# Forgetting attention without the row's constant and from the last block to the first, low key parts over zeros, and four output projection units in two pairs

## The chip, the cores and the metric

The kernel runs on one core of a Trainium2 chip. Its five engines run their own instruction queues: TensorE (PE: matmuls and transposes, with weight loads, PEld, beside them), VectorE (DVE), ScalarE (ACT), GpSimd (POOL) and SyncE (SP, which issues most DMAs). The metric is the device time of one execution, in microseconds; the time before is the median of three runs.

## The reference, cut to what matters

One decoder layer over 512 tokens of width 2048: a mixer, a cross-attention, a gated MLP, each behind an RMSNorm. The mixer has 12 dilated attention heads (A), 8 forgetting heads (B) and 4 heads of gated linear attention (C); their outputs, 2048 wide, go through one output projection. The forgetting heads:

```python
def forgetting_attention(q, k, v, f_logit):
    c = jnp.cumsum(jax.nn.log_sigmoid(f_logit.astype(jnp.float32)), axis=1)
    ...
    def block(args):                         # a block of 128 queries
        n, qn, cn = args
        logits = jnp.einsum('bihd,bjhd->bhij', qn, k, ...) * HEAD_DIM ** -0.5
        logits = logits + (cn[..., :, None] - cT[..., None, :])
        qpos = n * BLOCK_Q + jnp.arange(BLOCK_Q)
        logits = jnp.where(kpos[None, :] <= qpos[:, None], logits, -jnp.inf)
        p = jax.nn.softmax(logits, axis=-1)
        return jnp.einsum('bhij,bjhd->bihd', p.astype(v.dtype), v)
    ...
# hybrid_mixer:
    mixed = jnp.concatenate([o_a..., o_b..., o_c...], axis=-1)
    return mixed @ w_out
```

The term `cn` is one constant for each query, that is for each row of a softmax, and a softmax doesn't change when a constant is added to its row.

## The kernel before

**Products.** A float32 operand is split into a rounded high part and a low remainder (`xhi`/`xlo`, `whi`/`wlo`), ACT writing the high one and DVE the low one, and `mm3` (L375 to L377) issues three matmuls for each product of 128x128 weights with up to 512 columns: high by high, high by low, low by high. Tiles named `acc` are the PSUM accumulators of these foreground products, four in turn; all other PSUM tiles (`psS` scores, `psT` transposes, `psO` outputs) share four buffers of another tag.

**Foreground and background.** The foreground runs units: one unit takes a 128x1024 piece of weights by one DMA on SP (`wraw`), splits it in two halves and issues 24 matmuls. Attention heads, gates and the like are Python generators in `self.bg`; `tick` after every 12 foreground matmuls advances the first two of them by `self.rate` steps, one step being what stands between two `yield`s. PE instructions of a generator are put behind the last foreground matmul issued (`behind`). So the order on every engine is made by the generators' steps, and a scheduler orders the instructions of an engine from there.

**A head** (`attend`, L514 to L581). First step: query and key of the head are laid out over 128 partitions, `kh` with the rounded key in both halves (L526, L527) and `kl` with the low remainder in both (L529 by DVE, L530 a copy by ACT). Then eight steps, `scores` and `turn` of four blocks of 128 queries; block t has 128(t + 1) keys. `scores(t)`: two matmuls (L544, L545), one DVE operation that adds the bias and finds the row's maximum (L547), ACT's exponential with the row's sum (L548), a reciprocal (L549) and the scaling (L550). `turn(t)`: t + 1 transposes (L557), then `pth` by ACT (L565) and `ptl` by DVE (L566), at most two blocks at a time. The last step multiplies with the values (`psO`, L576 and L577) and writes the mixed stream (L579, L580).

**The bias of a forgetting head** (`bias_b`). `cb` (tile name `ba`) is the row of negative cumulative sums, the same in all partitions; for each block DVE makes a tile `bb`: `cb` minus the query's own constant `ci` (L599, L600), with the causal mask `self.tri` added to the last 128 columns (L600). The constants come from `forget`, which after the scan transposes the sums by four small PE transposes (L708) into `cnat` (L711). Five empty steps stand between scan and transposes.

**The gates** (`gates`): four heads' matmuls (L678), each followed by a DVE chain; they run as background together with `forget`, and `rel_bias` (L738) follows. **The output projection** has 16 units of two halves (`out_units`): the first halves of units 0 to 3 run while the last forgetting heads are in the background, the second halves behind them. Mixed tile k is split when a unit first asks for it (`mtile`).

Of the kernel before, what the change touches and what calls it, by code (L numbers as in the profile page):

```python
# [12 lines left out]
F32 = mybir.dt.float32  # L13
F32R = mybir.dt.float32r
I32 = mybir.dt.int32
AF = mybir.ActivationFunctionType
ALU = mybir.AluOpType
AX = mybir.AxisListType

P = 128  # L20
D = 2048
KT = D // P
S = 512
NT = S // P
# [3 lines left out]
DH = 64  # L28
A_HEADS = 12
B_HEADS = 8  # L30
# [37 lines left out]
PTB = 4  # L68
WR = 5
# [23 lines left out]
SB = 2  # L93
# [140 lines left out]
class _Trunk:  # L234
# [143 lines left out]
        if mark:  # L378
            self.last = last

    def out_units(self, src, nt, xs, evac, n=S):
        box = {}
        halves = len(xs) // 8

        def unit(half):
            if half == 0:
                box["ps"] = self.acc()
            w = self.weights(src[nt * halves + half])
            for kk in range(8):
                k = half * 8 + kk  # L390
                wh, wl = w(kk * P, P)
                self.mm3(box["ps"][:, :n], wh, wl, xs[k][0], xs[k][1], k == 0, k == len(xs) - 1)
                if kk == 3:
                    self.tick()
            if half == halves - 1:
                evac(box["ps"])

        return [lambda h=h: unit(h) for h in range(halves)]

# [118 lines left out]
    def attend(self, qf, kf, e, vv, bias_of, head, mix):  # L518
# [2 lines left out]
        o = slice(DH - DH * e, 2 * DH - DH * e)  # L521
        qs = ab.tile([P, S], F32R, name="qs", tag="qs", bufs=SB)
        kh = ab.tile([P, S], F32R, name="kh", tag="kh", bufs=SB)
        kl = ab.tile([P, S], F32R, name="kl", tag="kl", bufs=SB)
        nc.scalar.activation(qs[a], qf[a], AF.Copy)
        nc.scalar.activation(kh[a], kf[a], AF.Copy)  # L526
        nc.scalar.activation(kh[o], kf[a], AF.Copy)  # L527
        nc.vector.tensor_tensor(qs[o], qf[a], qs[a].bitcast(F32), op=ALU.subtract)
        nc.vector.tensor_tensor(kl[a], kf[a], kh[a].bitcast(F32), op=ALU.subtract)  # L529
        nc.scalar.activation(kl[o], kl[a].bitcast(F32), AF.Copy)  # L530
        yield
        pth = ab.tile([P, 1280], F32R, name="pth", tag="pth", bufs=PB)
        ptl = ab.tile([P, 1280], F32R, name="ptl", tag="ptl", bufs=PB)
# [32 lines left out]
                    nc.vector.tensor_tensor(lv, tv, hv.bitcast(F32), op=ALU.subtract)  # L566

        for f, t in ((scores, 0), (scores, 1), (turn, 0), (scores, 2), (turn, 1), (scores, 3), (turn, 2), (turn, 3)):
            f(t)
            yield  # L570
        po = self.pst("O")
        for b in range(NT):
# [17 lines left out]
    def bias_b(self, h):  # L590
        nc = self.nc
        cb = self.ab.tile([P, S], F32, name="ba", tag="ba", bufs=2)
        nc.scalar.dma_start(out=cb, in_=bass.AP(self.cdr.tensor, self.cdr.offset + h * S, [[0, P], [1, S]]))

        def get(t):
            b = self.ab.tile([P, P * (t + 1)], F32, name="bb", tag="pt", bufs=PTB, padded_shape=[P, S])
            ci = self.cnat[:, t, h:h + 1]
            if t:
                nc.vector.tensor_scalar(b[:, :P * t], cb[:, :P * t], ci, None, op0=ALU.subtract)  # L599
            nc.vector.scalar_tensor_tensor(b[:, P * t:], cb[:, P * t:P * (t + 1)], ci, self.tri,  # L600
                                           op0=ALU.subtract, op1=ALU.add)
            return b

        return get

# [80 lines left out]
    def forget(self):  # L686
        nc, gl = self.nc, self.pre
        fb = self.con.tile([B_HEADS, 1], F32, name="fb")
        with self.tc.issue_after(self.begun.ins):
            nc.gpsimd.dma_start(out=fb, in_=self.d["f_bias"])  # L690
        tp = self.pst("T")
        for t in range(NT):
            nc.tensor.transpose(tp[:B_HEADS, t * P:(t + 1) * P], self.fg[:, t, :B_HEADS], self.ident)
        z = gl.tile([B_HEADS, S], F32, name="fz", tag="zs", bufs=1)
        nc.vector.tensor_scalar(z, tp[:B_HEADS, :], fb, None, op0=ALU.add)
        n = self.neg_log_sigmoid(z, [B_HEADS, S])
        one = gl.tile([B_HEADS, S], F32, name="fone", tag="zs", bufs=1)
        nc.gpsimd.memset(one, 1.0)
        cn = gl.tile([B_HEADS, S], F32, name="cn")
        nc.vector.tensor_tensor_scan(cn, one, n, 0.0, ALU.mult, ALU.add)  # L700
        self.cdr = self.dr.tile([B_HEADS, S], F32, name="cdr")
        nc.scalar.dma_start(out=self.cdr, in_=cn)
        for _ in range(5):
            yield
        tq = self.pst("T")
        with self.behind():
            for t in range(NT):
                nc.tensor.transpose(tq[:, t * B_HEADS:(t + 1) * B_HEADS], cn[:, t * P:(t + 1) * P],  # L708
                                    self.ident[:B_HEADS, :B_HEADS])
        self.cnat = self.con.tile([P, NT, B_HEADS], F32, name="cnat")  # L710
        nc.vector.tensor_copy(self.cnat, tq[:, :NT * B_HEADS].rearrange("p (t h) -> p t h", h=B_HEADS))  # L711
        yield

    def rel_bias(self):
# [178 lines left out]
    def mixer(self):  # L893
# [91 lines left out]
        es_gl.close()  # L985
        self.mab = self.pool(self.es, "mab", "left")
        self.ab = self.pool(es_ab, "ab", "right")
        self.up_pre = {}
        for f in range(2, EARLY):
            self.up_sums(f)  # L990
# [18 lines left out]
        def evac_o(dt):  # L1009
            def f(ps):  # L1010
                self.resid(dt, ps, None, sqs, lambda n: self.mp.tile([P, n], F32, name="sqt", tag="sqt", bufs=2))
            return f
# [5 lines left out]
            def __getitem__(s, k):  # L1018
                return mtile(k)

        units = [self.out_units(d["w_o"], n, Lazy(), evac_o(n)) for n in range(KT)]
        self.rate = W_O / 2
        for n in range(4):
            units[n][0]()
            self.tick()
        self.rate = 0
        self.flush()
        es_ab.close()
# [832 lines left out]
```

## Time and profile before

| | |
|---|---|
| median of three runs | 2253.88 us (2253.62 to 2257.49) |
| the profiled execution | 2255.07 us, of which the span is 2253.3 us |
| busy PE / DVE / ACT / POOL | 2233.6 / 1824.1 / 1243.1 / 220.8 us |
| mean granted TensorE clock | 0.998 of full speed |
| gates and cumulative sums | 50 to 75 us of the span |
| dilated and forgetting heads | 330 to about 685 us |
| first halves of output units 0 to 3 | about 640 to 680 us |

Times count from the span's start. Matmuls are pipelined: one of 512 columns is shown with about 0.39 us, though the next starts 0.23 us later, so waits are read both from the idle time shown and from start to start. Idle time of an engine is put down to the last releaser. A line such as `psT<-ident,pt` reads output, arrow, inputs.

### The profile page before, as it was taken

What the parts mean: (1) busy time and instruction counts of PE and PEld (TensorE: products, weight loads), DVE (VectorE), ACT (ScalarE), POOL (GpSimd) and SP (SyncE); (2) the same over time, 40 slices, a digit from 0 to 9 for tenths busy, and PEclk for the clock granted to TensorE, in tenths of its full rate; (3) what the DMA queues carried; (4) which work ended last, traced back from release to release, by engine and by line L of the source; (5) the groups of instructions that cost most, each with busy time, mean ns of one, the idle gap of its engine ahead of it and who ended that gap; (6) DMA issues with size and microseconds to landing.
All of it is one profiled execution on the core that took longest, in us unless ns stands there. A gap on an engine that the chain in (4) does not pass through costs nothing.

```text
span 2253.3 us, 42653 instructions
## 1 busy us (share of the span) xinstructions
PE 2233.6 (99%) x15902; PEld 2090.3 (93%) x15902; DVE 1824.1 (81%) x3610; ACT 1243.1 (55%) x2552; POOL 220.8 (10%) x308
## 2 busy tenths in 40 slices
PE   9999999999999999999999999999999999999997
PEld 9898898888778888889999999999999999999997
DVE  7826756666797356699999999999999998999887
ACT  7324445655575245585555555555555575747563
POOL 2000101000002011121111111111000020101003
PEclk9999999999999999999999999999999999999999
DMA  6432157322223349589777777877534493836532
GB/s 223 158 98 83 50 149 192 97 89 99 81 88 129 133 151 251 124 207 273 197 212 209 209 211 214 225 221 218 180 132 143 143 337 106 306 127 234 186 129 82
DMA packets 141843, 377.10 MB, mean 167 GB/s; under 512 B 14484, under 2 KB 53732, under 8 KB 140932
## 3 DMA queue, kind: packets, MB, share of 16 engines
q1 hardware_dynamic: 90144, 274.18, 35.0%
q0 software_dynamic: 45728, 89.86, 18.2%
q10 hardware_dynamic: 5764, 10.35, 1.4%
q8 instruction: 124, 2.03, 0.4%
q14 instruction: 83, 0.68, 0.1%
HBM read 347.28 MB, written 91.80 MB: 195 GB/s over the span
## 4 chain that ended last, share of the span: by engine, by line
PE 95%; DVE 2%; ACT 1%; issue 1%; DMA 1%; POOL 0%; DVEq 0%; POOLq 0%; ACTq 0%
PE acc L375 19%; PE acc L377 19%; PE acc L376 19%; PE psC L375 5%; PE psC L376 5%; PE psC L377 5%; PE acc L416 3%; PE acc L418 3%; PE acc L417 3%; PE psD L376 3%; PE psD L375 3%; PE psD L377 3%; PE psT L557 1%; PE psQ L375 1%; PE psS L807 1%; PE psQ L377 1%
## 5 line engine op out<-in xcount | busy, mean ns | idle before, releaser
L336 ACT ACTIVATE whi<-wraw 128x512 fp32r<-128x512 f32 (+2 forms) x814 | 466.3, 603 | 406.6 <-PE acc L376 149.4
L337 DVE TENSOR_TENSOR wlo<-wraw,whi 128x512 fp32r<-128x512 f32 (+2 forms) x814 | 517.0, 656 | 66.8 <-ACT whi L336 62.1
L375 PE MATMUL acc<-sum,whi 128*128 128x256 f32 x1956 | 541.8, 277 | 0.4 <-ACT s L1461 0.3
L377 PE MATMUL acc<-sum,wlo 128*128 128x256 f32 x1956 | 541.6, 277 | 0.3 <-DVE wlo L337 0.2
L376 PE MATMUL acc<-sum,whi 128*128 128x256 f32 x1956 | 541.3, 277 | 0.0
L362 DVE TENSOR_TENSOR wlo<-wraw,whi 128x512 fp32r<-128x512 f32 (+2 forms) x336 | 221.0, 664 | 188.6 <-ACT whi L361 187.6
L377 PEld LDWEIGHTS acc<-sum,wlo 128*128 128x128 f32 x1956 | 367.3, 188 | 1.2 <-DVE wlo L337 1.1
L375 PEld LDWEIGHTS acc<-sum,whi 128*128 128x128 f32 x1956 | 367.1, 188 | 1.2 <-ACT s L1461 0.7
L376 PEld LDWEIGHTS acc<-sum,whi 128*128 128x128 f32 x1956 | 367.3, 188 | 0.0
L361 ACT ACTIVATE whi<-wraw 128x512 fp32r<-128x512 f32 (+2 forms) x336 | 203.0, 609 | 290.7 <-PE acc L376 176.1
L375 PE MATMUL acc<-xhi,whi 128*128 128x512 f32 (+1 forms) x848 | 335.1, 395 | 0.5 <-ACT fg L938 0.5
L377 PE MATMUL acc<-xhi,wlo 128*128 128x512 f32 (+1 forms) x848 | 328.3, 387 | 0.0
L376 PE MATMUL acc<-xlo,whi 128*128 128x512 f32 (+1 forms) x848 | 328.3, 387 | 0.0
L375 PE MATMUL psC<-sum,whi 128*128 128x256 f32 x928 | 256.8, 277 | 0.0
L376 PE MATMUL psC<-sum,whi 128*128 128x256 f32 x928 | 256.7, 277 | 0.0
L377 PE MATMUL psC<-sum,wlo 128*128 128x256 f32 x928 | 256.4, 276 | 0.0
L377 PEld LDWEIGHTS acc<-xhi,wlo 128*128 128x128 f32 x848 | 159.3, 188 | 32.3
L375 PEld LDWEIGHTS acc<-xhi,whi 128*128 128x128 f32 x848 | 159.4, 188 | 29.5 <-ACT fg L938 0.9
L376 PEld LDWEIGHTS acc<-xlo,whi 128*128 128x128 f32 x848 | 159.7, 188 | 28.4 <-DVE xlo L324 0.2
L376 PEld LDWEIGHTS psC<-sum,whi 128*128 128x128 f32 x928 | 174.2, 188 | 0.0
L377 PEld LDWEIGHTS psC<-sum,wlo 128*128 128x128 f32 x928 | 174.2, 188 | 0.0
L375 PEld LDWEIGHTS psC<-sum,whi 128*128 128x128 f32 x928 | 174.2, 188 | 0.0
(406 smaller groups left out, 4340.9 us busy)
## 6 DMA issues: line engine op xcount, KB each, us to landing
wraw<-in_w_up SPq DMA_DIRECT2D x125, 512.0 KB, 6.5
b<-in_w_up SPq DMA_DIRECT2D x42, 512.0 KB, 4.9
wraw<-in_w_o SPq DMA_DIRECT2D x32, 512.0 KB, 3.5
wraw<-in_w_d SPq DMA_DIRECT2D x32, 448.0 KB, 4.4
wraw<-in_w_d SPq DMA_DIRECT2D x36, 384.0 KB, 5.4
wraw<-in_w_qka SPq DMA_DIRECT2D x24, 512.0 KB, 3.6
up<-in_w_up POOLq DMA_DIRECT2D x24, 512.0 KB, 7.3
one<-in_w_d POOLq DMA_DIRECT2D x24, 448.0 KB, 7.3
```

The lines of the kernel that those rows point to most:

```text
L336: nc.scalar.activation(hi, r, AF.Copy)
L337: nc.vector.tensor_tensor(lo, r, hi.bitcast(F32), op=ALU.subtract)
L361: nc.scalar.activation(hi, r, AF.Copy)
L362: nc.vector.tensor_tensor(lo, r, hi.bitcast(F32), op=ALU.subtract)
L375: nc.tensor.matmul(out, lh, rh, start=start, stop=False, skip_group_check=more)
L376: nc.tensor.matmul(out, lh, rl, start=False, stop=False, skip_group_check=more)
L377: last = nc.tensor.matmul(out, ll, rh, start=False, stop=stop, skip_group_check=more)
L416: self.nc.tensor.matmul(o, xh[:, tt], wh, start=(k == 0), stop=False)
L417: self.nc.tensor.matmul(o, xh[:, tt], wl, start=False, stop=False)
L418: self.last = self.nc.tensor.matmul(o, xl[:, tt], wh, start=False, stop=(k == KT - 1))
L557: nc.tensor.transpose(tp[:, b * P:(b + 1) * P], pt[:, b * P:(b + 1) * P], self.ident)
L807: nc.tensor.matmul(sc[:rows, c * 64:(c + 1) * 64], kk[:, c * P:c * P + rows], qe[:, c * 64:(c + 1) * 64], start=True, stop=True)
```

## The change

**Forgetting heads.** The bias is `cb` plus the mask, with no constant of the row: `get(t)` adds `self.tri` in place on the 128 columns of block t and hands out `cb` up to there. Since the addition is in place, blocks go from the last (512 keys) to the first (128 keys); columns below t are still without the mask when block t reads them. `forget` loses its transposes, the copy and the five empty steps. **Low keys.** Two fixed tiles `self.kl[e]`, one for each head of a pair, have one half of the partitions set to zero once; a head writes the other half, and ACT's copy is gone from all 20 heads. The query tile has its high part in the one half and its low part in the other, so the low key now meets the high query alone. **Output projection.** The first halves of units 0 and 1, then of 2 and 3, run together: both weight pieces are asked for, and each mixed tile k is used by six matmuls in a row. The ticks stay at one for 12 matmuls.

```diff
@@ -378,22 +378,22 @@
         if mark:
             self.last = last
 
-    def out_units(self, src, nt, xs, evac, n=S):
-        box = {}
+    def out_units(self, src, nt, xs, evac, n=S, box=None):
+        box = {} if box is None else box
         halves = len(xs) // 8
 
         def unit(half):
             if half == 0:
-                box["ps"] = self.acc()
+                box[nt] = self.acc()
             w = self.weights(src[nt * halves + half])
             for kk in range(8):
                 k = half * 8 + kk
                 wh, wl = w(kk * P, P)
-                self.mm3(box["ps"][:, :n], wh, wl, xs[k][0], xs[k][1], k == 0, k == len(xs) - 1)
+                self.mm3(box[nt][:, :n], wh, wl, xs[k][0], xs[k][1], k == 0, k == len(xs) - 1)
                 if kk == 3:
                     self.tick()
             if half == halves - 1:
-                evac(box["ps"])
+                evac(box.pop(nt))
 
         return [lambda h=h: unit(h) for h in range(halves)]
 
@@ -521,13 +521,12 @@
         o = slice(DH - DH * e, 2 * DH - DH * e)
         qs = ab.tile([P, S], F32R, name="qs", tag="qs", bufs=SB)
         kh = ab.tile([P, S], F32R, name="kh", tag="kh", bufs=SB)
-        kl = ab.tile([P, S], F32R, name="kl", tag="kl", bufs=SB)
+        kl = self.kl[e]
         nc.scalar.activation(qs[a], qf[a], AF.Copy)
         nc.scalar.activation(kh[a], kf[a], AF.Copy)
         nc.scalar.activation(kh[o], kf[a], AF.Copy)
         nc.vector.tensor_tensor(qs[o], qf[a], qs[a].bitcast(F32), op=ALU.subtract)
         nc.vector.tensor_tensor(kl[a], kf[a], kh[a].bitcast(F32), op=ALU.subtract)
-        nc.scalar.activation(kl[o], kl[a].bitcast(F32), AF.Copy)
         yield
         pth = ab.tile([P, 1280], F32R, name="pth", tag="pth", bufs=PB)
         ptl = ab.tile([P, 1280], F32R, name="ptl", tag="ptl", bufs=PB)
@@ -566,7 +565,7 @@
                     nc.vector.tensor_tensor(lv, tv, hv.bitcast(F32), op=ALU.subtract)
 
         for f, t in ((scores, 0), (scores, 1), (turn, 0), (scores, 2), (turn, 1), (scores, 3), (turn, 2), (turn, 3)):
-            f(t)
+            f(t if bias_of == self.bias_a else NT - 1 - t)
             yield
         po = self.pst("O")
         for b in range(NT):
@@ -593,13 +592,9 @@
         nc.scalar.dma_start(out=cb, in_=bass.AP(self.cdr.tensor, self.cdr.offset + h * S, [[0, P], [1, S]]))
 
         def get(t):
-            b = self.ab.tile([P, P * (t + 1)], F32, name="bb", tag="pt", bufs=PTB, padded_shape=[P, S])
-            ci = self.cnat[:, t, h:h + 1]
-            if t:
-                nc.vector.tensor_scalar(b[:, :P * t], cb[:, :P * t], ci, None, op0=ALU.subtract)
-            nc.vector.scalar_tensor_tensor(b[:, P * t:], cb[:, P * t:P * (t + 1)], ci, self.tri,
-                                           op0=ALU.subtract, op1=ALU.add)
-            return b
+            b = cb[:, P * t:P * (t + 1)]
+            nc.vector.tensor_tensor(b, b, self.tri, op=ALU.add)
+            return cb[:, :P * (t + 1)]
 
         return get
 
@@ -700,15 +695,6 @@
         nc.vector.tensor_tensor_scan(cn, one, n, 0.0, ALU.mult, ALU.add)
         self.cdr = self.dr.tile([B_HEADS, S], F32, name="cdr")
         nc.scalar.dma_start(out=self.cdr, in_=cn)
-        for _ in range(5):
-            yield
-        tq = self.pst("T")
-        with self.behind():
-            for t in range(NT):
-                nc.tensor.transpose(tq[:, t * B_HEADS:(t + 1) * B_HEADS], cn[:, t * P:(t + 1) * P],
-                                    self.ident[:B_HEADS, :B_HEADS])
-        self.cnat = self.con.tile([P, NT, B_HEADS], F32, name="cnat")
-        nc.vector.tensor_copy(self.cnat, tq[:, :NT * B_HEADS].rearrange("p (t h) -> p t h", h=B_HEADS))
         yield
 
     def rel_bias(self):
@@ -985,6 +971,9 @@
         es_gl.close()
         self.mab = self.pool(self.es, "mab", "left")
         self.ab = self.pool(es_ab, "ab", "right")
+        self.kl = [self.ab.tile([P, S], F32R, name="kl%d" % e) for e in range(2)]
+        for kl, o in zip(self.kl, (slice(DH, P), slice(0, DH))):
+            nc.vector.memset(kl[o].bitcast(F32), 0.0)
         self.up_pre = {}
         for f in range(2, EARLY):
             self.up_sums(f)
@@ -1018,11 +1007,24 @@
             def __getitem__(s, k):
                 return mtile(k)
 
-        units = [self.out_units(d["w_o"], n, Lazy(), evac_o(n)) for n in range(KT)]
+        xo, box = Lazy(), {}
+        units = [self.out_units(d["w_o"], n, xo, evac_o(n), box=box) for n in range(KT)]
         self.rate = W_O / 2
-        for n in range(4):
-            units[n][0]()
-            self.tick()
+        for n in range(0, 4, 2):
+            raws = []
+            for i in range(2):
+                raws.append(self.wp.tile([P, 1024], F32, name="wraw", tag="wraw", bufs=WR))
+                nc.sync.dma_start(out=raws[i], in_=d["w_o"][2 * (n + i)])
+                box[n + i] = self.acc()
+            for half in range(2):
+                w = [self.split_weights(r[:, 512 * half:512 * (half + 1)]) for r in raws]
+                for kk in range(4):
+                    k, c = 4 * half + kk, slice(kk * P, (kk + 1) * P)
+                    for i in range(2):
+                        wh, wl = w[i]
+                        self.mm3(box[n + i], wh[:, c], wl[:, c], *xo[k], k == 0, False)
+                    if kk % 2:
+                        self.tick()
         self.rate = 0
         self.flush()
         es_ab.close()
```

What this makes of the order, at three places. In the changed file lines above 530 are the same or one lower, and the later ones some lines lower or higher (L599 and L600 become L596, L678 becomes L673, L738 becomes L724).

PE at the gates before (`g` and `w` are the gate product's operands, `cn` the sums of the forgetting heads, `acc` the foreground):

```order
257 L376 MATMUL acc<-xlo,whi 128x512
258 L377 MATMUL acc<-xhi,wlo 128x512
259 L678 MATMUL psO<-g_676,w_667 96x512
260 L708 MATMUL psT<-ident,cn 128x8 x4
261 L375 MATMUL acc<-xhi,whi 128x512
262 L376 MATMUL acc<-xlo,whi 128x512
```

This is the second of the four gate matmuls; the first stands at row 234 and the relative bias at 301 and 302. PE at the first gate matmul after:

```order
229 L376 MATMUL acc<-xlo,whi 128x512
230 L673 MATMUL psO<-g_676,w_667 96x512
231 L377 MATMUL acc<-xhi,wlo 128x512
232 L375 MATMUL acc<-xhi,whi 128x512
233 L376 MATMUL acc<-xlo,whi 128x512
234 L377 MATMUL acc<-xhi,wlo 128x512
235 L724 MATMUL psO<-ohr,tbr 12x512
236 L724 MATMUL psO<-ohr,tbr 12x128
```

The first gate matmul moves up by four rows, the relative bias from 301 to 235, and the other gate matmuls follow at rows 249, 262 and 275, twelve foreground matmuls apart.

ACT at the end of the second forgetting pair before, where the next pair's keys are laid out (`kf` is the key as projected, `pth` the turned probabilities that psO needs):

```order
464 L526 ACTIVATE kh<-kf 64x512
465 L579 ACTIVATE ot<-psO 64x512
466 L565 ACTIVATE pth<-psT 128x2x128
467 L527 ACTIVATE kh<-kf 64x512
468 L530 ACTIVATE kl<-kl 64x512
469 L526 ACTIVATE kh<-kf 64x512
470 L565 ACTIVATE pth<-psT 128x128
471 L527 ACTIVATE kh<-kf 64x512
472 L361 ACTIVATE whi<-wraw 128x512
473 L565 ACTIVATE pth<-psT 128x2x128
474 L530 ACTIVATE kl<-kl 64x512
475 L565 ACTIVATE pth<-psT 128x256
```

And ACT at the same place after:

```order
450 L526 ACTIVATE kh<-kf 64x512
451 L527 ACTIVATE kh<-kf 64x512
452 L578 ACTIVATE ot<-psO 64x512
453 L564 ACTIVATE pth<-psT 128x2x128
454 L526 ACTIVATE kh<-kf 64x512
455 L527 ACTIVATE kh<-kf 64x512
456 L361 ACTIVATE whi<-wraw 128x512
457 L564 ACTIVATE pth<-psT 128x128
```

The kl copies are gone, and of the `pth` copies around the next pair's keys two are left where there were four, the last of them 128 columns wide.

DVE in the same pair before (`wlo` is a foreground split; ISA is the operation that adds the bias and finds the maximum):

```order
958 L599 TENSOR_SCALAR bb<-ba,cnat 128x384
959 L550 TENSOR_SCALAR pt<-pt,sm 128x128
960 L600 SCALAR_TENSOR_TENSOR bb<-ba,cnat,tri 128x128
961 L362 TENSOR_TENSOR wlo<-wraw,whi 128x512
962 L547 ISA pt,nm<-psS,bb 128x512
963 L547 ISA nm 128x1
```

And DVE in it after:

```order
966 L546 ISA pt,nm<-psS,ba 128x256
967 L546 ISA nm 128x1
968 L596 TENSOR_TENSOR ba<-ba,tri 128x128
969 L579 TENSOR_TENSOR str<-psO,ot 64x512
970 L548 RECIPROCAL sm<-sm 128x1
971 L565 TENSOR_TENSOR ptl<-psT,pth 128x2x128
972 L549 TENSOR_SCALAR pt<-pt,sm 128x256
973 L546 ISA pt,nm<-psS,ba 128x128
```

A block's bias is one operation instead of up to two, and a head's last blocks are the narrow ones.

## The prediction

> **What bounds the kernel now.** I read the page's shares first, then the chain that ended last, then what TensorE waited for, then stretches of time, and last the places of the longest waits, row by row.
>
> ```profile
> span 2253.3 us, 42653 instructions
> PE 2233.6 (99%) x15902; PEld 2090.3 (93%) x15902; DVE 1824.1 (81%) x3610; ACT 1243.1 (55%) x2552; POOL 220.8 (10%) x308
> ...
> PE 95%; DVE 2%; ACT 1%; issue 1%; DMA 1%; POOL 0%; DVEq 0%; POOLq 0%; ACTq 0%
> ```
>
> TensorE (PE) is busy 99% of the span and carries 95% of the chain. An edit that shortens VectorE (DVE) or ScalarE (ACT) work pays only where PE stands still for it. The list of PE's waits in the whole program, total, times, longest:
>
> ```profile
> PE psO L576 <- ACT pth L565: 1.8, 2, 1.5
> ...
> PE psT L557 <- DVE pt L550: 0.9, 3, 0.4
> ...
> PE psS L545 <- ACT kl L530: 0.4, 1, 0.4
> ```
>
> These three rows are what the change can reach: 1.8 + 0.9 + 0.4 = 3.1 us. The rest of the list, none over 1.0 us, lies at the program's start and behind the mixer. Next, busy time by stretches (columns: PE, weight loads, DVE, ACT, POOL, granted clock, DMA share, GB/s). The first two hold the gates and the forgetting bias's cumulative sum; 395 to 680 runs from dilated heads into forgetting heads, and 655 to 680 has the last heads under the first output projection units.
>
> ```profile
> 50.00:60.00 10.00, 10.00 (x50) 8.07 (x49) 9.59 (x16) 4.11 (x7) 0.98 (x2) 1.00 0.15 54
> 60.00:75.00 15.00, 15.00 (x67) 11.81 (x66) 14.84 (x26) 4.95 (x8) 0.00 (x0) 1.00 0.19 71
> ...
> 555.00:632.00 77.00, 75.34 (x370) 61.91 (x369) 58.15 (x163) 48.08 (x109) 0.00 (x0) 1.00 0.26 87
> 632.00:655.00 23.00, 22.95 (x111) 18.81 (x110) 20.98 (x61) 18.00 (x43) 0.00 (x0) 1.00 0.23 80
> 655.00:680.00 25.00, 23.80 (x120) 18.95 (x119) 23.44 (x69) 16.18 (x40) 0.00 (x0) 1.00 0.21 77
> ...
> 395.00:680.00 285.00, 282.09 (x1382) 233.80 (x1382) 207.51 (x574) 175.41 (x413) 0.00 (x0) 1.00 0.26 90
> ```
>
> PE idles 285.00 - 282.09 = 2.9 us in all of 395 to 680: 1.66 in 555 to 632 and 1.20 in 655 to 680. DVE is 94% busy in the latter (23.44 of 25) and 98% busy in 50 to 75 (24.43 of 25), where PE nevertheless never idles. So 0.2% of the span, 4.5 us, which is about what a measurement of this kernel can tell from no change, is more than all the idle time that the change touches.
>
> **The change, part by part.** Prices of one instruction, from the groups by shape in 495 to 680 us:
>
> ```profile
> L600 DVE SCALAR_TENSOR_TENSOR bb<-ba,cnat,tri 128x128 f32<-128x128 f32 x30 | 10.3, 343 | 0.0
> L599 DVE TENSOR_SCALAR bb<-ba,cnat 128x384 f32<-128x384 f32 x7 | 2.9, 409 | 0.0
> L599 DVE TENSOR_SCALAR bb<-ba,cnat 128x256 f32<-128x256 f32 x7 | 2.4, 347 | 0.0
> L599 DVE TENSOR_SCALAR bb<-ba,cnat 128x128 f32<-128x128 f32 x8 | 2.3, 282 | 0.0
> L566 DVE TENSOR_TENSOR ptl<-psT,pth 128x128 fp32r<-128x128 f32 x20 | 5.7, 284 | 1.4 <-ACT pth L565 1.2
> L566 DVE TENSOR_TENSOR ptl<-psT,pth 128x256 fp32r<-128x256 f32 x42 | 17.3, 417 | 3.6 <-ACT pth L565 3.5
> L547 DVE CUSTOM_DVE_ANT_0 pt<-psS,bb 128x512 f32<-128x512 f32 x7 | 4.8, 683 | 1.2 <-PE psS L545 1.2
> L547 DVE CUSTOM_DVE_ANT_0 pt<-psS,bb 128x128 f32<-128x128 f32 x8 | 2.3, 284 | 0.4 <-PE psS L545 0.3
> ...
> L530 ACT ACTIVATE kl<-kl 64x512 fp32r<-64x512 f32 x10 | 6.3, 628 | 1.1 <-DVE kl L529 1.0
> L548 ACT ACTIVATE pt<-pt,nm 128x512 f32<-128x512 f32 x11 | 8.0, 724 | 2.6 <-DVE nm L547 2.3
> L548 ACT ACTIVATE pt<-pt,nm 128x128 f32<-128x128 f32 x10 | 4.0, 402 | 3.7 <-DVE nm L547 3.6
> ```
>
> *Bias.* A forgetting head loses three tensor_scalars, 0.41 + 0.35 + 0.28 = 1.04 us of DVE, and turns four 343 ns operations into plain additions of the same size. The nearest row for these is the 128x128 tensor_tensor at 284 ns, though it reads PSUM once, so 4 x 0.06 = 0.24 more is saved: 1.28 a head, 10.2 us for eight. All of it is DVE time beside matmuls; it counts only through waits.
>
> The Trainium skill ("VectorE: DVE Perf Modes", section "Mode 2×_2P — use both read ports for one tensor") speaks against such a swap: an fp32 tensor_scalar in SBUF delivers two elements a cycle and a tensor_tensor one. The rows agree: from 128 to 384 columns the one kind grows by (409 - 282) / 256 = 0.50 ns a column, from 128 to 256 the other by (417 - 284) / 128 = 1.04. Were the whole width swapped, a head's four blocks would be 0.28 + 0.42 + 0.55 + 0.68 = 1.9 us as tensor_tensors against 2.4 now, still no loss; but the wide part isn't swapped here, it is dropped.
>
> *Low keys over zeros.* ACT loses one 628 ns copy in each of 20 heads, 12.6 us, off the chain but for the bursts below. The two memsets before the heads are 64x512 on DVE, at most the 628 ns of the same shape each, at about 320 us. In 110 to 330 DVE has 220.0 - 120.5 us of room by the row below, and PE no idle time, so 0; without that cover 1.3 us.
>
> ```profile
> 110.00:330.00 220.00, 220.00 (x1255) 203.05 (x1254) 120.50 (x340) 84.36 (x190) 15.69 (x17) 1.00 0.29 92
> ```
>
> The psS row above is the first pair's wait for the copy. Without the copy, PE comes to the second head's key instead, whose ACT copies end at about the same time: 0, with -0.4 as the bound.
>
> *Row constants.* Four small transposes and their copy go:
>
> ```profile
> L708 PE MATMUL psT<-ident,cn x4: 201/202/223, 59.2 to 59.4; 8*128 8x8 f32 x4
> ```
>
> The first starts at 59.2 and the last at 59.4, so they hold some 0.3 us of PE. With five empty steps gone from that generator, the gate matmuls and the relative bias come up to 24 matmuls earlier, while DVE is 98% busy. By the order of rows and the ends of their producers in the timeline, an estimate, PE's first gate matmul arrives 0.4 us before the DVE operation that it needs is done; the last one is also close, since it needs the PSUM reader of the second. I put +0.3 against -0.3: 0. Bounds: -0.3, and +1.3 if both are late by what I find at the closest. The skew's two DMAs on ACT's queue move up by some 20 us too, into stretches with a DMA share of 0.19; their first reader comes after 330 us.
>
> *Last to first.* Here is the longest wait, on PE and then on ACT:
>
> ```profile
> 594.78 0.60 PE L557 MATMUL psT<-ident,pt 128*128 128x128 f32 x4
> 595.13 0.48 PE L375 MATMUL acc<-xhi,whi 128*128 128x512 f32 x1
> 595.45 0.40 PE L376 MATMUL acc<-xlo,whi 128*128 128x512 f32 x1
> 595.68 0.40 PE L377 MATMUL acc<-xhi,wlo 128*128 128x512 f32 x1
> 597.54 0.50 PE L576 MATMUL psO<-pth,vv 128*128 128x512 f32 x1 [1.46 <-ACT pth L565]
> ...
> 594.50 0.61 ACT L530 ACTIVATE kl<-kl 64x512 fp32r<-64x512 f32 x1
> 595.12 0.63 ACT L526 ACTIVATE kh<-kf 64x512 fp32r<-64x512 f32 x1
> 595.77 0.28 ACT L565 ACTIVATE pth<-psT 128x128 fp32r<-128x128 f32 x1
> 595.95 0.61 ACT L527 ACTIVATE kh<-kf 64x512 fp32r<-64x512 f32 x1
> ...
> 597.12 0.37 ACT L565 ACTIVATE pth<-psT 128x256 fp32r<-128x256 f32 x1
> ```
>
> A 512-column matmul takes its turn in 0.23 us (595.45 to 595.68), so 597.54 should have been 595.91; the wait is 1.63 from start to start. ACT is the cause: its queue runs key copies of the next pair ahead of the last pth. The new order drops from that burst the kl copy (595.12 - 594.50 = 0.62), one 128-column pth (595.95 - 595.77 = 0.18), and makes the last pth 128 columns instead of 256 (0.37 to 0.28, so 0.1): ACT is ready 0.9 earlier. But PE too comes earlier: of the last turns' seven transposes (three and four) it now has three (two and one), the others having moved ahead of the burst. Four hold PE from 594.78 to 595.13, 0.35. So 0.9 - 0.35 = 0.55, and I take -0.5; bounds 0 and the whole wait, -1.5.
>
> At the next pair's end a matmul holds its turn for 0.45 before psO's second operand:
>
> ```profile
> 632.78 0.40 PE L375 MATMUL acc<-xhi,whi 128*128 128x512 f32 x1
> 633.23 0.50 PE L577 MATMUL psO<-ptl,vv 128*128 128x512 f32 x1
> ```
>
> That is 0.22 too long, though the view calls none of it idle, and the psO ahead of it came about 0.1 late. A 128-column pth and ptl fit between the matmuls there: -0.3 (bounds 0, -0.3).
>
> In 655 to 680 the waits are those of the last heads:
>
> ```profile
> 665.98 0.44 PE L557 MATMUL psT<-ident,pt 128*128 128x128 f32 x2 [0.45 <-DVE pt L550]
> ...
> 667.62 0.50 PE L576 MATMUL psO<-pth,vv 128*128 128x512 f32 x1 [0.30 <-ACT pth L565]
> ```
>
> Before the last transposes of a head stands the 512-column chain: bias 0.41 + 0.34, scores plus bias 0.68, exponential 0.72. With the 128-column block last these are 0.28, 0.28 and 0.40, 1.2 us shorter, more than any single wait here. Idle is 1.2 us; with five places, each 0.17 longer from start to start as at 597, it is about 2.0. Two head ends give back 0.35 each of PE work that now lies earlier: 2.0 - 0.7 = 1.3, and I take -1.2. Bounds: 0 and -2.0.
>
> In return the first transposes of a head wait for the 512-column chain, 0.40 + 0.32 and a scaling, together about 0.9 longer than the 128-column one. Their cover is 24 matmuls of 0.23, 5.5 us, in most heads; the first forgetting head has 15 matmuls and I expect 0.2 to 0.4 there, against the idle of 555 to 632 beyond 597's, 1.66 - 1.46 = 0.2, and as much in late starts, which lies at that head's kl and goes: 0, bounds -0.4 and +0.9.
>
> *Output projection two by two.* The matmuls are the same 96, and the steps are issued at the same cadence, one per 12 matmuls. A mixed tile now serves six matmuls instead of three, so its split is asked for at half the pace; the pieces of weights are split by the same ACT and DVE instructions. On SP the two raws of a pair are asked for together, 32 transfers as before:
>
> ```profile
> wraw<-in_w_o SPq DMA_DIRECT2D x32, 512.0 KB, 3.5
> ```
>
> PE waits for no DMA in the list, and a pair's 48 matmuls last 11 us against 3.5 of landing: 0. If the second raw came late, its 3.5 us would show once or twice.
>
> *Sum:* -0.5 - 0.3 - 1.2 + 0 = -2.0 us on the profiled execution's 2255.07 (2253.3 of it span), so 2253.1. The median of the runs is 2253.88, 1.2 below that execution; on it the same sum gives **2251.9**.
>
> **The rivals.**
> *Slower: the wide block first leaves a head's first transposes bare.* If the DVE and ACT queues hold the 512-column chain (about 2.3 us by itself with its scaling) for over 5.5 us, each of eight heads pays up to the 0.9 by which it has become longer: 7.4 - 2.0 = +5.4, 2259.3. For it: the ACT burst held a 0.37 us copy back for 1.5 us, and DVE is over 90% busy from 632 on. Against it: only the last two pairs run under such load, and the DVE loses 1.28 us a head. It decides from 3.2 us of queueing per head.
>
> *Faster by over 4.5.* All 2.9 us of idle in 395 to 680 go, 0.4 at the first pair, 0.3 of the transposes, and PE's pace itself gets better: after a group of transposes the next 512-column matmul holds its turn for 0.32 (595.13 to 595.45) instead of 0.23 us, 0.09 x 32 groups of eight forgetting heads = 2.9. Together 6.5: 2247.4. Against it: the groups stay, in another order, so the last term has no reason in the change.
>
> *Nothing happens.* What is taken out of ACT and DVE is hidden, and the waits move with the blocks: the earlier transposes take back what the shorter copies give. 2253.9. For it: the 0.35 that I had to subtract at 597 is over a third of the gain there, and nine tenths of the DVE and ACT savings lie beside PE work.
>
> **How the numbers follow.** The forecast, 1 to 3.5 us less, has 0.60; nothing (within 1 us either way) 0.20; the faster rival 0.09; the slower one 0.06; 1 to 4.5 slower through the gates, the memsets or the weights' transfers 0.05. Faster by over 0.2% is 0.09, slower 0.06, and between them 0.85. The range takes the bounds that are likely together: down 0.5 + 0.8 + 0.4 + 0.8 from the forecast, to 2249.4; up to the profile's second case and the gates' +1.3, 2255.2. It leaves the two outer rivals out.
>
> **What would show it.** Right: psO's wait at the end of the second forgetting pair falls from 1.5 to about 1 us; idle of 655 to 680 falls from 1.2 to under 0.6; kl disappears from PE's waits; DVE has some 10 us and ACT 12.6 us less, with PE's busy time the same within 1 us. A wait for DVE at the gates, 50 to 75 us, of 0.3 to 0.4 would be new. Wrong: psT waiting for the scaled block (L549 after) in every head, which is the slower rival; any PE wait on a DMA in the output projection; or PE's busy time down by several us, which none of my terms contains.

## The result, and the profile after

The changed kernel takes 2290.5 us (median of 5, 2289.39 to 2290.59) against 2255.18 (5 runs): a ratio of 1.0155, interval 1.0141 to 1.0169, some 35 us slower. The forecast was 2251.9. The profiled execution of it has a span of 2287.6 us. The page's shares hardly move:

```profile
span 2287.6 us, 42608 instructions
PE 2270.0 (99%) x15898; PEld 2118.8 (93%) x15898; DVE 1822.5 (80%) x3587; ACT 1236.1 (54%) x2532; POOL 223.5 (10%) x308
...
PE 96%; DVE 2%; ACT 1%; issue 0%; DMA 0%; POOL 0%; DVEq 0%; ACTq 0%; POOLq 0%
```

PE is busy for 36.4 us more (2270.0 against 2233.6) with four instructions fewer. The waits that the change was to shorten did get shorter:

```profile
PE psW L258 <- POOL ones L255: 1.0, 1, 1.0
PE acc L377 <- DVE wlo L362: 0.8, 1, 0.8
PE acc L375 <- ACT fg L924: 0.6, 1, 0.6
PE psS L543 <- ACT kh L527: 0.5, 1, 0.5
PE psO L673 <- DVE g L667: 0.3, 1, 0.3
...
PE psO L575 <- ACT pth L564: 0.2, 1, 0.2
PE psT L556 <- DVE pt L549: 0.2, 1, 0.2
```

psO is at 0.2 instead of 1.8 us, psT at 0.2 instead of 0.9. So the loss is no wait. The stretches show where it is, after and then before (PE's count is the number in brackets):

```profile
110.00:330.00 220.00, 220.00 (x1246) 202.39 (x1245) 121.10 (x342) 83.43 (x188) 14.69 (x16) 1.00 0.28 88
...
1100.00:1400.00 300.00, 300.00 (x2570) 300.00 (x2570) 281.72 (x444) 163.29 (x291) 42.46 (x55) 1.00 0.76 208
1400.00:1700.00 300.00, 300.00 (x2571) 300.00 (x2570) 282.19 (x445) 163.54 (x292) 27.95 (x36) 1.00 0.67 190
```

```profile
1100.00:1400.00 300.00, 300.00 (x2638) 300.00 (x2638) 287.47 (x457) 165.27 (x296) 41.48 (x54) 1.00 0.78 216
1400.00:1700.00 300.00, 300.00 (x2638) 300.00 (x2637) 287.00 (x456) 167.24 (x299) 27.38 (x36) 1.00 0.67 193
```

From 1100 to 1700 us the MLP runs, of which the change touches nothing. In the same 600 us, with PE busy throughout and a granted clock of 1.00, it issues 5141 matmuls instead of 5276: each takes a turn (the time from its start to the next start) of 116.7 instead of 113.7 ns. The 110 to 330 us stretch has 1246 instead of 1255. A longer turn counts as busy time, so neither the waits nor the busy share can show it; the count in a full stretch does, and so do start times, here of the first and the last of six matmuls of the output projection in a row, after and then before:

```profile
701.74 0.40 PE L376 MATMUL acc<-xlo,whi 128*128 128x512 f32 x1
...
702.90 0.39 PE L375 MATMUL acc<-xhi,whi 128*128 128x512 f32 x1
```

```profile
701.82 0.39 PE L375 MATMUL acc<-xhi,whi 128*128 128x512 f32 x1
...
702.95 0.39 PE L377 MATMUL acc<-xhi,wlo 128*128 128x512 f32 x1
```

The turn is (702.90 - 701.74) / 5 = 0.232 us after and (702.95 - 701.82) / 5 = 0.226 before. Summed from start to start over the whole trace, 512-column matmuls (3039 of them) cost 721.9 us instead of 712.8, 384-column ones 117.2 instead of 116.2, and 256-column ones (11309) 1325.3 instead of 1300.7: 9.1 + 1.0 + 24.6 = 34.7 us. That is all of the loss (the totals hold PE's waits too, which shrank).

What reaches every matmul is not in the order of instructions. The row constants' tile `cnat` has 128 bytes in each partition. It stood ahead of the weight tiles on its side of SBUF. By the built programs' addresses, `whi` and `wlo` stand at 192 within 256 bytes before and at 64 after; the mixer's streaming operands `xhi` and `xlo`, on the other side, stay at 192, most of the MLP's streaming operands (its `sum` tiles) at 128. My theory was that the distance, the address of the weights less that of the stream within 256 bytes, sets the turn ("place"); its rival was that the new order or the new instructions slow the matmuls ("work").

### The profile page after: what moved, and what is told of

Same layout as the page of the kernel before. It is cut to its first block, busy times and chain, and to the rows that moved or that the text cites. A ratio compares the mean times of both kernels' runs of the same rounds, so it can differ in the third digit from the quotient of the medians.

```text
span 2287.6 us, 42608 instructions
## 1 busy us (share of the span) xinstructions
PE 2270.0 (99%) x15898; PEld 2118.8 (93%) x15898; DVE 1822.5 (80%) x3587; ACT 1236.1 (54%) x2532; POOL 223.5 (10%) x308
## 4 chain that ended last, share of the span: by engine, by line
PE 96%; DVE 2%; ACT 1%; issue 0%; DMA 0%; POOL 0%; DVEq 0%; ACTq 0%; POOLq 0%
PE acc L375 19%; PE acc L377 19%; PE acc L376 19%; PE psC L376 5%; PE psC L375 5%; PE psC L377 5%; PE acc L416 3%; PE acc L418 3%; PE acc L417 3%; PE psD L375 3%; PE psD L376 3%; PE psD L377 3%; PE psT L556 1%; PE psQ L377 1%; PE psQ L376 1%; PE psQ L375 1%
## 5 line engine op out<-in xcount | busy, mean ns | idle before, releaser
L336 ACT ACTIVATE whi<-wraw 128x512 fp32r<-128x512 f32 (+1 forms) x822 | 475.0, 603 | 427.5 <-DVE wraw L1433 160.1
L337 DVE TENSOR_TENSOR wlo<-wraw,whi 128x512 fp32r<-128x512 f32 (+1 forms) x822 | 523.9, 656 | 84.4 <-ACT whi L336 79.7
L362 DVE TENSOR_TENSOR wlo<-wraw,whi 128x512 fp32r<-128x512 f32 (+2 forms) x328 | 216.3, 665 | 199.9 <-ACT whi L361 198.4
L361 ACT ACTIVATE whi<-wraw 128x512 fp32r<-128x512 f32 (+2 forms) x328 | 198.6, 609 | 302.7 <-PE acc L376 188.5
```

The lines of the kernel that those rows point to most:

```text
L336: nc.scalar.activation(hi, r, AF.Copy)
L337: nc.vector.tensor_tensor(lo, r, hi.bitcast(F32), op=ALU.subtract)
L361: nc.scalar.activation(hi, r, AF.Copy)
L362: nc.vector.tensor_tensor(lo, r, hi.bitcast(F32), op=ALU.subtract)
```

## The experiments

**The changed kernel with the 128 bytes back.** One line in `forget`:

```diff
+        self.con.tile([P, 32], F32, name="spare")
```

> The changed kernel with an unused tile of 128 bytes a partition where the row constants' tile stood, so that every later SBUF tile on that side stands where it stood before the change; no instruction differs. Theory (place): the slower pace of all matmuls comes from the weight tiles standing 128 bytes lower, at 64 instead of 192 within 256 bytes, while the operands that stream stay. Then the 512-column turn goes back from 232 to 227 ns, the 256-column one from 117 to 113, and the time is what the three edits themselves make: 2252 to 2255 us. Rival (work): the new order or the new instructions slow the matmuls; then it stays at 2290.

Measured: 2254.45 us against 2256.01, ratio 0.9994 (0.9985 to 1.0003).

```profile
1100.00:1400.00 300.00, 300.00 (x2639) 300.00 (x2638) 287.50 (x456) 166.06 (x298) 41.71 (x54) 1.00 0.77 215
```

The MLP's pace is back (2639), with an edit that issues nothing. Place holds; what the three edits do by themselves can't be told from zero.

**The kernel before with 128 bytes more.** The same line behind `cnat`, and nothing of the change.

> The kernel before with nothing of the change, but 128 more unused bytes behind the row constants' tile; this puts the weight tiles at 64 within 256 bytes, as removing the tile did. Place: about +35 us, 2287 to 2293, with turns of 232 and 117 ns. Work: 2255, as nothing else differs.

Measured: 2291.64 us, ratio 1.0158 (1.0145 to 1.0172).

```profile
1100.00:1400.00 300.00, 300.00 (x2571) 300.00 (x2570) 281.67 (x443) 162.72 (x289) 40.97 (x53) 1.00 0.77 210
```

The whole loss without any of the change. The rival falls.

**The streams moved along.** The changed kernel, with the unused tile at the other end of SBUF larger by 128 bytes:

```diff
-        edge.tile([P, 8], F32, name="edge")
+        edge.tile([P, 40], F32, name="edge")
```

> The changed kernel with the unused tile at the other end of SBUF 128 bytes larger, so that activations and most other streaming operands move by 128 bytes too: weights and streams both stand at 64 within 256. Place, if the distance of weights and stream counts: back to 2252 to 2255. Place, if the weights' own position counts: 2290. Work: 2290.

Measured: 2253.27 us, ratio 0.9986 (0.9977 to 0.9996). Weights stand at 64 as in the slow kernel, and it is fast: the distance counts, not the place.

**Only the weights out of place.** The changed kernel with `self.mc.tile([P, 32], F32, name="spare")`, directly behind the weight tiles.

> The changed kernel with 128 unused bytes directly behind the weight tiles: everything on that side but the constants' last tiles and the weight tiles is back in its place, the weights stay at 64 within 256. Place (weights against stream): still 2288 to 2292. Rival (the vector operands that moved, such as the streams and sums, are what slows): 2252 to 2256.

Measured: 2283.92 us, ratio 1.0127 (1.0102 to 1.0151), but four runs from 2278.18 to 2291.75, a spread that no other kernel here has. The 512-column total is 722.7 us, as after; the 256-column one 1312.5 in the profiled execution, halfway. The weights' place costs the mixer's 9 us by itself; in the MLP something else takes part, which came out further below. By the programs' addresses its sums don't all stand alike in the two: eight of the 56 are at 0 in the changed kernel and at 128 here.

**Other distances.** The kernel before with `[P, 16]` and `[P, 48]` in the same place, weights at 0 and at 128.

> The kernel before with 64 more unused bytes ahead of the weight tiles, which puts them at 0 within 256 instead of 192; nothing else is changed. Place: slower than before, since the weights stand at +64 of the mixer's streams (192) and at 128 of the MLP's (128): the few rows of the traces so far with 512 columns at +64 have 226 to 230, and 256 at 128 away none; I expect 113 to 117 there, 2255 to 2295 us. Rival (only a shift by 128 matters): 2255.

> The kernel before with 192 more unused bytes ahead of the weight tiles, which puts them at 128 within 256; nothing else is changed. Place: the traces so far have 233 ns for 512 columns at this distance (100 matmuls) and 120 for 256 columns (263 matmuls); 2660 x 6 ns + 9900 x 6 ns = 16 + 59 us, so 2330. Rival (only a shift by 128 matters): 2255 or 2290.

Measured: 2310.9 us (ratio 1.0242, 1.0227 to 1.0258) and 2309.64 (1.0237, 1.0221 to 1.0252). Slower as expected, though I had put the one too low and the other 20 us too high: the 512-column total rises by 11.3 and 3.4 us, the 256-column one by 45.1 and 50.4.

**TensorE alone.** 96 matmuls for each of 32 combinations, no other engine at work.

> Nothing of the reference is computed: after one load and two copies TensorE alone runs 32 groups of 96 matmuls, 8 weight tiles in turn, with no other engine at work; groups differ only in where the weights stand within 256 bytes against the streaming operand (steps of 32 bytes), in the operand's own place (two places) and in its width (512, 384, 256 columns). Place, as a matter of TensorE's two reads alone: the turn of a 512-column matmul is 226 to 227 ns at distance 0 and 229 to 233 at others, that of 256 columns 113 at +64 and 117 to 120 at 0 and at -64, and it is the same for equal distances at both places of the operand. Rival (the weight tiles' writers, ACT, DVE and DMA, collide with TensorE's reads at some places): all 512-column groups run at one pace, all 256-column ones too.

From the starts of each group, ns a matmul, by the weights' distance from the stream within 256 bytes:

| distance | 0 | 32 | 64 | 96 | 128 | 160 | 192 | 224 |
|---|---|---|---|---|---|---|---|---|
| 512 columns, stream at 0 | 226.7 | 233.3 | 233.4 | 234.2 | 233.3 | 233.4 | 229.0 | 233.4 |
| 512 columns, stream at 128 | 226.7 | 233.3 | 233.4 | 234.2 | 232.3 | 233.4 | 229.0 | 233.3 |
| 384 columns, stream at 128 | 173.4 | 173.3 | 174.7 | 176.6 | 176.0 | 176.7 | 173.3 | 176.6 |
| 256 columns, stream at 128 | 119.9 | 118.3 | 117.8 | 117.3 | 120.0 | 119.9 | 117.8 | 117.8 |

(In the first group with the stream at 128, distance 0, the last 60 turns are taken, without the start-up.) Two of the groups with the stream at 0, distances 0 and 128, by tile, with the first and last start:

```profile
L1859 PE MATMUL qe<-x,w x96: 389/389/397, 278.7 to 300.3; 128*128 128x512 f32 x96
...
L1859 PE MATMUL qa<-x,w x96: 387/394/398, 189.6 to 211.7; 128*128 128x512 f32 x96
```

(300.3 - 278.7) / 95 = 227 ns at distance 0, (211.7 - 189.6) / 95 = 233 at 128. For 512 columns the table has the mixer's loss: with TensorE alone at work, the same at equal distance to within 1 ns, and 0, where the kernel before stands, is the best. The kernels' own traces agree: the medians of the 2448 such matmuls of `xhi` and `xlo` are 227 at distance 0 (before), 233 at 64 and 230 at 192 (the two versions above) and 232 at 128 (changed). The row for 256 columns was a miss: 113 doesn't appear at any distance. I repeated it in the kernel's pattern of three.

> As the first measurement of TensorE alone, but in the kernel's own pattern of three: high weights on the high stream, the same weights on the low stream, low weights on the high stream; nothing of the reference is computed. Groups: 512, 256 (operand at 128 and at 160 within 256... the second place is 128 bytes on, at 0) and 384 columns, weights at eight places each. Theory: the pattern of 256 columns, which came to 117 to 120 at every place when the weights changed each time, now shows 113 at a distance of +64, as in the MLP, and 117 or more at -64 and 0. Rival: TensorE alone never reaches 113 at 256 columns, and the MLP's pace has another cause. 512 columns: 227 at distance 0, 229 at -64, 231 to 234 elsewhere, as before.

Measured: the same to 0.1 ns at 256 columns for a stream at 128 (117.8 at +64), and up to 1.3 ns apart for one at 0. The rival seemed to hold.

**The MLP's sums all at one place.** Four of its 56 sum tiles stand at 96, by an unused tile of 32 bytes (`step`); I took that out.

> The changed kernel with the unused tile of 128 bytes, and without another unused tile of 32 bytes between the MLP's sums; four sums move from 96 to 128 within 256, where the others stand. Theory: their 840 matmuls go from 117 to 113 ns, -3 us: 2251 to 2252, ratio to before 0.998. Rival: the vector work beside them, which moves by 32 bytes too, slows by as much or more: 2254 or above.

Measured: 2282.68 us, ratio 1.0121 (1.0104 to 1.0138). A plain miss: all sums now stand at the distance of +64, and the pace in the MLP is lost over most of it.

```profile
1100.00:1400.00 300.00, 300.00 (x2550) 300.00 (x2549) 280.29 (x441) 161.83 (x288) 43.26 (x58) 1.00 0.77 211
```

Start times in the MLP gave the clue. Before, the six matmuls of a pair of tiles at 96 take 115 to 119 ns, the next four or so 115 to 120, and then all take 113 or 114 until the next such pair. Without such tiles they take 117 to 119 from 1036 to 2030 us, and mostly 113 or 114 behind that, at the same places. After the change, some stretches run at 113 and some at 118, and most keep their pace until the next such pair. So places alone don't make a pace: at this width there are two, each holds itself, and a few matmuls elsewhere may throw TensorE from one to the other.

**That alone.** 48 matmuls, then a few with the stream moved (the kick), then 90 as at first.

> TensorE alone, nothing of the reference: 24 groups of 256-column matmuls in the kernel's pattern of three, each 48 matmuls with fixed places, then 3 to 12 with the streaming operand elsewhere within 256 bytes, then 90 with the first places again; weights at +64 (a), -64 (b) or 0 (c) from the stream. Theory (two paces that hold themselves, and a few matmuls at another place throw TensorE from one into the other): the 48 before run at 117.8 everywhere; the 90 after stay at 117.8 where nothing was moved (first group of each letter), and drop to 113 to 114 in some of the others, for a move by -32 bytes at +64 as in the MLP above all. Rival (the pace of 113 needs something else in the MLP): all the 90s run at 117 to 120.

By tile: `pre`, `kick` and `post`, a for weights at +64, b at -64, c at 0, then a letter for the kick.

```profile
L1862 PE MATMUL pread<-x,w x48: 276/276/276, 60.1 to 65.5; 128*128 128x256 f32 x48
...
L1862 PE MATMUL kickad<-x,w x6: 277/280/285, 65.6 to 66.2; 128*128 128x256 f32 x6
...
L1862 PE MATMUL postad<-x,w x90: 279/281/281, 66.3 to 76.8; 128*128 128x256 f32 x90
...
L1862 PE MATMUL preae<-x,w x48: 281/281/281, 76.9 to 82.4; 128*128 128x256 f32 x48
...
L1862 PE MATMUL postae<-x,w x90: 276/276/283, 83.3 to 93.4; 128*128 128x256 f32 x90
```

Same weights, same stream: before a kick of +32 bytes 115 ns ((65.5 - 60.1) / 47 with rounded starts; 113.3 from the single starts), behind it (76.8 - 66.3) / 89 = 118, which holds into the next group, until a kick of +64 brings 113 back. At +64 six matmuls moved by -32, as in the MLP, left the pace at 113 and twelve turned it to 118; at -64 three moved by -32 turned it from 118 to 113, and there the five kicks of six ahead of them did nothing. At distance 0 all is at 120, whatever the kick. Two parts of the expectation were wrong: the first group came out of its start-up at 113, not 117.8, and the kick of the MLP, six by -32 at +64, didn't bring 113. It met 113 already; whether it turns 118 into 113 was not tested. Two paces that hold themselves are shown; which kick does what is a table without a rule.

**One kick instead of two.** The step moved behind the second of those four sums, so that one pair stands at 96:

```diff
-        put(sx, OFF)
+        put(sx, OFF[:2])
         sx.tile([P, HALF], F32, name="step")
-        put(sx, order)
+        put(sx, OFF[2:] + tuple(order))
```

> The changed kernel with the unused tile of 128 bytes, and the 32-byte tile two sums further on: two sums (six matmuls in each round of the MLP's products) stand at 96 within 256, two now at 128 with the rest. Theory of two paces: the one place that is left suffices to reach 113 and the pace then holds through the other sums; half of the 840 matmuls at 117 and of the four or so behind them gain 4 ns, -2 to -3 us against the version with both: 2251 to 2253. Rival (each stretch needs its own kick, or drops back at PSUM changes): half or more of the MLP's matmuls go to 117.7, as without the tile, and it takes 2265 to 2283.

Measured: 2251.64 us against 2255.39, ratio 0.9985 (0.9976 to 0.9994), as the theory had it: 0.15% under the kernel before, with a span of 2248.7. The 256-column total is 1296.6 us, 3.9 below that of the version with both; the ratios of the two versions (0.9994, 0.9985 to 1.0003) have intervals that overlap.

```profile
1100.00:1400.00 300.00, 300.00 (x2644) 300.00 (x2643) 288.13 (x457) 167.05 (x299) 41.70 (x54) 1.00 0.78 216
```

**The parts alone,** all tiles in their places: the forgetting heads with the unused 128 bytes, the low keys in the kernel before, the pairs in the kernel before.

> The forgetting heads' part alone (bias without the row's constant, blocks from last to first), with the unused tile of 128 bytes, so that all stands where it did; low keys and output projection as before. Theory: it takes most of the waits of 395 to 680 us (psO, psT), -1 to -1.5 us, ratio 0.9993 to 1.0. Rival: the parts undo one another, and this one alone gains over 2 or loses.

> The low keys over zeros alone, in the kernel before; all weights and streams stay where they were. Theory: ACT loses 12.6 us, and 0.3 to 1 us of TensorE's waits goes (the first pair's, a part of the one of 1.5 us at the second forgetting pair's end); ratio 0.9995, not to be told from 1. Rival: the matmuls over zeros run at another pace: a difference of more than 2 us either way.

> The output projection's first four units two by two, alone, in the kernel before; all tiles stay where they were. Theory: 0, within 1 us: the mixed tiles' splits are asked for at half the pace, which takes up to 0.5 us of waits in 655 to 680. Rival: two weight transfers at once come late, with a wait of TensorE for a DMA or a weight split of 1 to 3 us.

Measured: 1.0002 (0.9993 to 1.0011), 0.9997 (0.9988 to 1.0006) and 0.9996 (0.9987 to 1.0006). None can be told from 1. The waits tell more; PE's wait for psO in each, in that order:

```profile
PE psO L576 <- ACT pth L565: 1.6, 1, 1.6
```

```profile
PE psO L575 <- ACT pth L564: 0.9, 1, 0.9
```

```profile
PE psO L576 <- ACT pth L565: 1.5, 1, 1.5
```

The reversed blocks alone leave the wait at 1.6 us (before, 1.5), against their expectation; dropping the kl copy alone takes it to 0.9; with all three parts it is 0.2. Blocks and low keys without the pairs were not run. In 655 to 680 us PE idled 1.20 before. The forgetting heads alone and the pairs alone leave:

```profile
655.00:680.00 25.00, 24.19 (x124) 19.63 (x123) 22.63 (x66) 17.58 (x42) 0.00 (x0) 1.00 0.32 106
```

```profile
655.00:680.00 25.00, 24.66 (x124) 19.77 (x123) 23.90 (x74) 17.69 (x44) 0.00 (x0) 1.00 0.21 74
```

That is 0.81 and 0.34: the pairs take more of the idle time there than the reversed blocks.

## Why the prediction was wrong

**The step that failed** is *Row constants*. It priced the tile's transposes, its copy and the five steps, and left out that a tile is also 128 bytes ahead of the weight tiles. Moving the weights by these 128 bytes, with nothing of the change, made the kernel before slower by a ratio of 1.0158, as much as the whole change (1.0155). The sum had no term for PE's pace, and "PE's busy time down by several us, which none of my terms contains" was named as a sign of error only in the other direction. The faster rival spoke of the pace, took it from the one matmul behind a group of transposes, and said itself that the change gave the term no reason. None of the rivals had a mechanism outside the mixer, though the MLP's PE time is more than half of the span. The clock was 0.998 in all the whole kernels and is no part of it. The signs of being right among the waits held in the changed kernel (psO's wait 0.2 us, idle of 655 to 680 0.10, no wait for kl, a new one of 0.3 at the gates). Those of busy time didn't: PE's was to stay within 1 us and rose by 36.4, DVE's and ACT's fell by 1.6 and 7.0 for 10 and 12.6 (by 6.6 and 11.9 with the bytes back).

**The terms of the sum** can be read from the version with the bytes put back, in which pace is as before. PE's idle time by stretches (length less PE's busy time), before and in that version:

| stretch, us | before | with the bytes | the step |
|---|---|---|---|
| 50 to 85 | 0 | 1.20 | gates, bound +1.3 |
| 330 to 395 | 0.39 | 0.52 | first pair, 0 |
| 555 to 632 | 1.66 | 0.34 | second pair's end, -0.5 |
| 632 to 655 | 0.05 | 0 | -0.3 |
| 655 to 680 | 1.20 | 0.14 | last heads, -1.2 |
| 680 to 700 | 0 | 0.18 | none |

The first stretch before, and then three of the version with the bytes:

```profile
50.00:85.00 35.00, 35.00 (x159) 28.17 (x158) 34.24 (x57) 13.07 (x22) 1.51 (x3) 1.00 0.19 67
```

```profile
50.00:85.00 35.00, 33.80 (x149) 26.80 (x149) 29.79 (x49) 11.56 (x20) 0.98 (x2) 1.00 0.41 154
...
555.00:632.00 77.00, 76.66 (x375) 62.70 (x373) 55.83 (x154) 45.89 (x105) 0.00 (x0) 1.00 0.27 91
...
655.00:680.00 25.00, 24.86 (x125) 20.06 (x124) 22.69 (x68) 16.02 (x40) 0.00 (x0) 1.00 0.27 83
```

- *Last to first*: the sizes came out at the last heads, -1.06 of idle for -1.2, but with all three parts. By themselves the forgetting heads take 0.39 there, so the near number is in part luck: the pairs, put at 0, take 0.86 alone. At the second pair's end it is -1.3 for -0.5: I subtracted transposes that had moved ahead of the burst, yet the wait fell from 1.46 to 0.21, near the far bound. Alone, the reversed blocks take nothing of it and the kl copy about half; why they give more together is not shown.
- *Row constants*, its gate part: the new wait at the first gate matmul is there, 0.3 for 0.4. But a second one came that I hadn't seen: PE stands 0.87 us for a foreground weight split, queued on DVE behind a gate's 1.22 us scan. My bound of +1.3 was for another case, two late gate matmuls, and that 1.20 lies within it is luck. It is half of what the heads gained in the three stretches from 555 to 680, 2.43.

```profile
52.61 0.45 PE L673 MATMUL psO<-g,w 112*96 112x512 f32 x1 [0.33 <-DVE g L667]
...
83.89 0.50 PE L377 MATMUL acc<-xhi,wlo 128*128 128x512 f32 x1 [0.87 <-DVE wlo L362]
```

- *Low keys*: 0 at the first pair was right; it waits 0.5 for a key copy instead of 0.4 for kl. The copies' gain lies in the burst, as above.
- *Bias*: the additions cost 283 ns each (395 to 680 us), where I took 284 from the nearest row. What I hadn't seen: the first addition of the first forgetting head starts 3 us after the DMA of `cb` is issued (544.3 to 547.3), where the first bias operation before came 18 us after (543.3 to 561.7). So DVE waits for that DMA, hidden from PE.

```profile
L596 DVE TENSOR_TENSOR ba<-ba,tri 128x128 f32<-128x128 f32 x31 | 8.7, 283 | 4.2 <-DMA ba<-cdr 4.2
```

- *Output projection*: alone 0.9996 of the time, not to be told from the forecast 0; by its idle time, above, it is more than 0, and no wait for a DMA came.

The spans' difference, 2253.3 to 2251.9, is -1.4 us for the -2.0 of the sum, and the runs' ratio of 0.9994 holds both. *The slower rival* is out: the first transposes of a head don't wait with the wide block first (psT 0.2 us in all). Its price had a slip: eight heads at 0.9 are 7.2, not 7.4.

The Trainium skill ("TensorE: Matmul & The Clock Gate", section "Wait — 56ns, not 53.3ns?") gives a warm matmul's turn by its width alone, N / 2.4 GHz and about 2.5 ns. Here (fp32 in its rounded form) 512 columns took 226.7 to 234.2 ns and 256 columns 113.3 to 120.0 with nothing changed but the operands' places; the measurements decide.

## What to carry to other kernels

When a tile goes, comes or changes its size, compare the addresses of what stands behind it, not the instructions alone: first the distance, within 256 bytes, between weights and streaming operand. When PE is full, compare the number of matmuls in equal stretches of the two traces, in a stage that the change doesn't touch; a slower pace shows as busy time, and no list of waits has it. A part of a change that is tested by itself should leave every other tile where it was, if need be by an unused tile of the size that was removed.

## What the runs showed that I had not expected

- TensorE's turn depends on where weights and stream stand to each other: at 512 columns 226.7 ns at distance 0, 229.0 at 192 and 232 to 234 at others, with no other engine at work.
- At 256 columns and a distance of 64 either way there are two paces, 113.3 and 117.8 ns, with the same operands. Each holds over 90 matmuls and into the next group, and 3 to 12 matmuls at another place can switch them. In the kernel the 256-column matmuls have 24.6 of the 35 us, in stretches at 113 and at 118.
- With only the weights out of place, executions of one kernel lay between 2278.18 and 2291.75 us. That fits two paces, but which stretch of which execution ran at which was seen in one profile only. Why there are two, and which kick turns which way, stays open.
- Distance alone isn't the whole rule at 512 columns either: by the programs' addresses 96 matmuls of the kernel before with `mhi` and `mlo` as weights stand at 192; they take 233 to 234 (medians), where TensorE alone has 229; with the streams moved along, still at 192, they take 226 to 232. That stays open too.
